# Query projections of a cross attention as seven-product units, with operands made by the output projection and partly kept in DRAM

## The chip, the cores and the metric

One core of one Trainium2 chip runs the whole program. The metric is the device time of one execution in microseconds (us), smaller being better. The engines are TensorE (PE: matmuls; PEld: its weight loads), VectorE (DVE), ScalarE (ACT), GpSimd (POOL) and SyncE (SP), which issues nearly all transfers from one queue, in order.

## The reference, cut to what matters

One layer of a trunk, D = 1024, 1024 tokens, in float32. The part that is changed is the output projection of the mixing block and the cross attention behind it:

```python
x = x + merged @ w_out[i].astype(dt)
h = rmsnorm(x, norm_xattn_g[i])
m = rmsnorm(mem.astype(dt), norm_mem_g[i])
q = (h @ xattn_wq[i].astype(dt)).reshape(bsz, seq, XATTN_HEADS, XATTN_HEAD_DIM)
...
s = jnp.einsum('bshd,bmhd->bhsm', q, k).astype(f32) * (XATTN_HEAD_DIM ** -0.5)
p = jax.nn.softmax(s, axis=-1).astype(dt)
o = jnp.einsum('bhsm,bmhd->bshd', p, v).reshape(bsz, seq, D_MODEL)
x = x + o @ xattn_wo[i].astype(dt)
```

There are 4 heads of 256 columns and 256 memory tokens. In front of this stand two recurrent branches and their merge, behind it a squared-ReLU MLP and a last norm.

## The kernel before

**Arithmetic.** Everything is feature-major: a tile has 128 features as partitions and 512 tokens (a *half*) as its free axis, and x is 8 blocks by 2 halves, in the slots A0a (half 0) and A0b (half 1). A float32 product is made of three fp32r matmuls (`mm3`, L519, L521, L523): both operands are split in a rounded high part (`split`: ACT, L559) and a low rest (DVE or POOL, L560), and high x high, high x low and low x high are summed in PSUM.

**Units of seven products.** The branch projections, the attention's output projection (`pu` below) and the MLP take 256 output columns and all 1024 tokens as a 2x2 problem of blocks and use a Winograd form of Strassen's scheme: seven products p = 0 to 6 of 4 blocks of 128 each, so 7 x 4 x 3 = 84 matmuls of 512 columns for what otherwise takes 96. `wino_w` makes the seven weight operands (sums, then splits, into tiles `wop`, a ring of 4); `blocks` makes the seven operands of the other side from four blocks b00, b01, b10, b11 (row block, half): it sinks b00 (0), b10 (1), b11 (5), then overwrites in place b11-b01 (4), b01-b00 (3), their sum T (2) and b10-T (6). `direct` splits an operand into its slot at once, `spill` writes it to DRAM, from where `load_op` reads it into a small staging tile (`rawa`, two buffers, or `e`) and splits it.

**The output projection** (`phase_out`) is plain: per unit u of 256 columns 96 matmuls; L1875 adds a block to x, L1876 writes the high part of g*x (ACT) and L1859 the low part (DVE), straight into the operand slots of the queries, and the squares for the norm are summed (L624 to L628). The norm's factor is applied later, in the softmax (`rsc`).

**The attention** (`phase_attn`). `queries(h, half)` makes one head's queries for one half: 48 matmuls in 2 blocks of 128, evicted and split (L1920, L1921) into `qt`, which is slot B0b. These eight generators are the *fill*: `scores(h, g)` emits, for each of four blocks of 128 tokens, six matmuls of 256 columns and a softmax (L1947 to L1955), then `SF` = 11 fill matmuls. Within it `flush` finishes the group before: transposes of the probabilities (L591), their split (L1931, L1932), `PF0` = 4 fill matmuls, 12 matmuls with v, and the blocks of the result (L1940) go to `pd` in DRAM (heads 0 to 2) or into the operand slots (head 3). Half 0 of head 0 is made ahead of the first scores; the other seven half-heads fill the groups up to and with scores(3, 0). Scores(3, 1), the eighth group, has none. Then `pu` runs, two units at a time, each twice 84 matmuls; `into_x` (L1707, L1712, L1719) adds to x, and its operand slots are A1a, A1b, B0a, t4, B0b, B1a, B1b. B0b, B1a and B1b hold `qt`, the transposed probabilities and the keys and values until the last flush.

**Order.** The program is traced once; then `Plan` simulates all engines with costs per instruction and writes an order for each engine by due times (four rounds, the best is kept). On PE it takes the earliest traced matmul that is ready, so later matmuls move into gaps; two-input sums marked as flexible go to DVE or POOL. On the chip each engine then runs its list in order.

Of the kernel before, what the change touches and what calls it, by code (L numbers as in the profile page):

```python
# [18 lines left out]
P = 128  # L19
# [29 lines left out]
SF, PF0 = 11, 4  # L49

# [399 lines left out]
class Layer:  # L450
# [186 lines left out]
    def consts(self):  # L637
# [22 lines left out]
        self.gneg = self.til(cp, [P, NB, GH], "gneg")  # L660
# [186 lines left out]
    def decay_cols(self, gb):  # L847
        nc = self.nc
        pt = self.pss()
        for c in range(NB):  # L850
            nc.tensor.transpose(pt[:, c * 64:(c + 1) * 64], gb[:, c * P:(c + 1) * P], self.ident[:64, :64])
        nc.vector.tensor_copy(self.tm, pt.rearrange("p (a b c) -> p a b c", b=2, c=32)[:, :, :, 0:GH])
        nc.scalar.activation(self.geg, self.tm[:, :, 0], AF.Exp)
        nc.vector.tensor_scalar(self.gneg, self.geg, -1.0, None, MUL)
# [354 lines left out]
    def gdn_keys(self, sp, sq, h, st):  # L1209
# [14 lines left out]
        nb = self.til(sq, [P, NB], "nb", bufs=2)  # L1224
# [107 lines left out]
    def gdn_scan(self, sp, hs, sts, nfill):  # L1332
# [4 lines left out]
        for c in range(NB):  # L1337
            zh, qs, dl, pd = {}, {}, {}, {}
            for h, st in hs:
# [8 lines left out]
                nc.vector.scalar_tensor_tensor(zh[h], pa[:, 0:P], self.gneg[:, c, h:h + 1], v[:, c, :], MUL, ADD)  # L1348
# [4 lines left out]
            for h, st in hs:  # L1353
# [3 lines left out]
                nc.scalar.activation(dl[h], py[:, 0:P], AF.Copy, scale=st["b"][:, c:c + 1])  # L1357
# [164 lines left out]
    def op_tile(self, ops, p):  # L1522

        if p not in ops:
            n = self.SL[p]
            ops[p] = self.til(self.lp, [P, 2, 4, HALF], n, F32R, bufs=1) if n == "t4" else self.slot(n, (2, 4, HALF))
# [6 lines left out]
    def staged(self, sp, src, both=True):  # L1533
# [5 lines left out]
        return raw  # L1539

# [310 lines left out]
    def phase_out(self, sp):  # L1851
# [3 lines left out]
        h2 = self.h2 = {}  # L1855

        def lo_in(blk, half):
            g, x = self.g_x[:, blk:blk + 1], self.xT[half][:, blk]
            nc.vector.scalar_tensor_tensor(h2[half][1][:, blk], x, g, h2[half][0][:, blk].bitcast(F32), MUL, SUB)  # L1859

        h2[0] = [self.slot("A1a"), self.slot("A1b")]
        h2[1] = [self.til(self.lp, [P, 2, 4, HALF], "t4", F32R, bufs=1).rearrange("p a b t -> p (a b) t")]

        def out(u):
            w = self.plain_w()
            yield
            for i in range(2):
                blk = 2 * u + i
                for half in range(2):
                    hi, lo = self.mT[half]  # L1870
                    pt = self.psd()
                    yield from self.mm3(pt, [((w[i, b % 2][:, 0, b // 2], w[i, b % 2][:, 1, b // 2]), (hi[:, b], lo[:, b]))
                                             for b in (0, 1, 2, 3, 4, 6, 5, 7)])
                    x = self.xT[half][:, blk]
                    nc.vector.scalar_tensor_tensor(x, pt, 0.5, x, MUL, ADD)  # L1875
                    nc.scalar.activation(h2[half][0][:, blk], x, AF.Copy, scale=self.g_x[:, blk:blk + 1])  # L1876
                    if half == 0:
                        lo_in(blk, half)
                    sq(blk, half)
# [4 lines left out]
        h2[1].append(self.slot("B0a"))  # L1884
        for blk in range(NB):
            lo_in(blk, 1)


    def phase_attn(self, sp):
        nc = self.nc  # L1890
        sc = 1.0 / 16.0
        h2 = self.h2
        rs, pend, puts, op = {}, [], {}, {}
        pd = lambda p, k: self.pd[p][:, k]
        self.SL = ("A1a", "A1b", "B0a", "t4", "B0b", "B1a", "B1b")
        qt, pT, kv = self.slot("B0b", (2, 2, 2, HALF)), self.slot("B1a", (2, 2, 2, HALF)), self.slot("B1b", (2, 2, 2, 2, MEM))
# [11 lines left out]
        qw = {}  # L1908

        def queries(h, half):  # L1910
            if half == 0:
                qw[h] = self.plain_w()
            w = qw[h]
            for i in range(2):
                hi, lo = h2[half]
                pt = self.psd()
                yield from self.mm3(pt, [((w[i, b % 2][:, 0, b // 2], w[i, b % 2][:, 1, b // 2]), (hi[:, b], lo[:, b]))
                                         for b in (0, 1, 2, 3, 4, 6, 5, 7)])
                q = qt[:, half, :, i]
                nc.scalar.activation(q[:, 0], pt, AF.Copy)  # L1920
                nc.vector.tensor_tensor(q[:, 1], pt, q[:, 0].bitcast(F32), SUB)  # L1921

        def flush():
# [3 lines left out]
            n = (2 * h + g) % 2  # L1927
            for mb in range(2):
                pt = self.transpose4([e[:, mb * P:(mb + 1) * P] for e in ps])
                t = pT[:, n, :, mb]  # L1930
# [4 lines left out]
            for i in range(2):  # L1935
                pt = self.psd()
                fs = slice(i * P, (i + 1) * P)
                self.all3(pt, [((v[:, 0, mb, fs], v[:, 1, mb, fs]), (pT[:, n, 0, mb], pT[:, n, 1, mb])) for mb in range(2)])
# [21 lines left out]
        def scores(h, g):  # L1960
            k, ps = kv[:, 0, h % 2], []
            for i in range(4):
                pt = self.pss()
                ts = slice(i * P, (i + 1) * P)
                self.all3(pt[:, :MEM], [((qt[:, g, 0, b, ts], qt[:, g, 1, b, ts]), (k[:, 0, b], k[:, 1, b])) for b in range(2)])
# [6 lines left out]
        for h in range(XH):  # L1972
            for half in range(2):
                self.push(f"q{h}{half}", queries(h, half))
# [4 lines left out]
        self.until("q00")  # L1979
        for h in range(XH):  # L1980
            for g in range(2):
# [3 lines left out]
                self.until(f"q{h + g}{1 - g}")  # L1985
                if h == XH - 1:
                    for p in ((0, 1, 2), (3,))[g]:
                        self.load_op(sp, op, p, pd, range(XH - 1), False)
        self.mo = {}
# [14 lines left out]

        flush()
        for p in (4, 5, 6):
            self.load_op(sp, op, p, pd, range(XH - 1), False)
# [257 lines left out]
    def run(self):  # L2265
# [11 lines left out]
        self.gcd = dt([GH, T], "gcd")  # L2277
        self.dmd = [dt([P, T], f"dmd{h}") for h in range(GH)]
# [44 lines left out]
        with ExitStack():  # L2323
            self.phase_merge(sp, ob)
            self.phase_out(sp)
# [100 lines left out]
```

## Time and profile before

| | |
|---|---|
| Time, median of 3 runs (lowest to highest) | 2171.57 us (2170.28 to 2173.66) |
| Profiled execution: time / span | 2173.49 us / 2171.7 us |
| PE, DVE, ACT, POOL busy | 98%, 76%, 51%, 8% of the span |
| DMA, mean | 142 GB/s |
| Output projection / attention / `pu` | about 1232 to 1314 / 1314 to 1462 / 1462 to 1541 us |

The span runs from the first to the last instruction; the profiled execution took 1.8 us more than its span. A busy PE is not PE at its peak, since matmuls overlap: the pitch from start to start counts, not the length of one.

### The profile page before, as it was taken

What the parts mean: (1) busy time and instruction counts of PE and PEld (TensorE: products, weight loads), DVE (VectorE), ACT (ScalarE), POOL (GpSimd) and SP (SyncE); (2) the same over time, 40 slices, a digit from 0 to 9 for tenths busy, and PEclk for the clock granted to TensorE, in tenths of its full rate; (3) what the DMA queues carried; (4) which work ended last, traced back from release to release, by engine and by line L of the source; (5) the groups of instructions that cost most, each with busy time, mean ns of one, the idle gap of its engine ahead of it and who ended that gap; (6) DMA issues with size and microseconds to landing.
All of it is one profiled execution on the core that took longest, in us unless ns stands there. A gap on an engine that the chain in (4) does not pass through costs nothing. (4 is left out here: it accounts for less than half of the span.)

```text
span 2171.7 us, 31058 instructions
## 1 busy us (share of the span) xinstructions
PE 2138.2 (98%) x11064; PEld 1811.3 (83%) x11064; DVE 1660.2 (76%) x3001; ACT 1103.3 (51%) x2199; POOL 181.4 (8%) x209
## 2 busy tenths in 40 slices
PE   8999999999999999999999999999999999999998
PEld 7789889888888888888888888887888888888877
DVE  7869988885778879685689844469989778567766
ACT  6445545543656464655444434565655556444433
POOL 0001010101112110210000000001101000000011
PEclk9999999999999999999999999999999999999999
DMA  8422323223121211221768621345354445688852
GB/s 303 178 74 94 109 93 127 88 83 134 38 69 64 78 55 48 63 84 63 263 225 303 223 97 62 112 151 172 116 190 129 159 156 178 194 266 287 279 184 93
DMA packets 145308, 308.54 MB, mean 142 GB/s; under 512 B 15865, under 2 KB 19321, under 8 KB 145153
## 3 DMA queue, kind: packets, MB, share of 16 engines
q1 hardware_dynamic: 142256, 302.33, 42.5%
q10 hardware_dynamic: 2896, 4.22, 0.5%
q8 instruction: 87, 1.43, 0.3%
q14 instruction: 69, 0.56, 0.1%
HBM read 216.54 MB, written 89.95 MB: 141 GB/s over the span
## 5 line engine op out<-in xcount | busy, mean ns | idle before, releaser
L559 ACT ACTIVATE wop<-raw 128x512 fp32r<-128x512 f32 (+1 forms) x465 | 303.5, 659 | 469.8 <-PE pd L523 223.9
L560 DVE TENSOR_TENSOR wop<-raw,wop 128x512 fp32r<-128x512 f32 (+1 forms) x439 | 316.0, 723 | 117.1 <-ACT wop L559 111.0
L523 PE MATMUL pd<-t,wop 128*128 128x512 f32 x296 | 117.7, 397 | 0.2 <-DVE wop L560 0.2
L519 PE MATMUL pd<-t,wop 128*128 128x512 f32 x296 | 115.9, 391 | 1.2 <-DVE u L1707 1.2
L523 PE MATMUL pd<-A1a,wop 128*128 128x512 f32 (+1 forms) x292 | 111.1, 381 | 0.0
L519 PE MATMUL pd<-A1a,wop 128*128 128x512 f32 (+1 forms) x292 | 111.0, 380 | 0.0
L1174 DVE SCALAR_TENSOR_TENSOR acc<-cin,convw,acc 128x1024 f32<-128x1024 f32 x72 | 92.2, 1280 | 5.1 <-ACT acc L1172 4.7
L521 PE MATMUL pd<-t,wop 128*128 128x512 f32 x232 | 90.5, 390 | 0.0
L521 PE MATMUL pd<-A1a,wop 128*128 128x512 f32 (+1 forms) x228 | 85.5, 375 | 0.0
L521 PE MATMUL pd<-A1b,wop 128*128 128x512 f32 x212 | 83.1, 392 | 0.0
L560 DVE TENSOR_TENSOR wlo<-raw,whi 128x512 fp32r<-128x512 f32 x59 | 40.2, 687 | 42.2 <-ACT whi L559 41.4
L521 PE MATMUL pd<-B0a,wop 128*128 128x512 f32 x176 | 69.0, 392 | 0.0
L559 ACT ACTIVATE whi<-raw 128x512 fp32r<-128x512 f32 x68 | 41.9, 627 | 52.7 <-PE pd L521 45.4
L519 PE MATMUL pd<-B0a,wop 128*128 128x512 f32 x176 | 68.6, 390 | 0.0
L523 PE MATMUL pd<-B0a,wop 128*128 128x512 f32 x176 | 68.6, 390 | 0.0
L521 PE MATMUL pd<-B0b,wop 128*128 128x512 f32 x176 | 68.5, 389 | 0.0
L521 PE MATMUL pd<-B1b,wop 128*128 128x512 f32 x172 | 66.9, 389 | 0.0
L519 PEld LDWEIGHTS pd<-t,wop 128*128 128x128 f32 x296 | 55.7, 188 | 12.5 <-DVE u L1707 2.0
L523 PEld LDWEIGHTS pd<-t,wop 128*128 128x128 f32 x296 | 55.7, 188 | 11.6 <-DVE wop L560 0.7
L519 PEld LDWEIGHTS pd<-A1a,wop 128*128 128x128 f32 x292 | 55.1, 189 | 9.8
L523 PEld LDWEIGHTS pd<-A1a,wop 128*128 128x128 f32 x292 | 55.0, 188 | 9.6
L1171 ACT ACTIVATE cin<-pd 128x512 f32<-128x512 f32 x48 | 28.5, 594 | 67.5 <-PE pd L523 67.4
(613 smaller groups left out, 6676.0 us busy)
## 6 DMA issues: line engine op xcount, KB each, us to landing
raw<-in_w_dram SPq DMA_DIRECT2D x120, 256.0 KB, 3.7
raw<-in_w_dram SPq DMA_DIRECT2D x32, 512.0 KB, 4.2
e<-ad SPq DMA_DIRECT2D x63, 256.0 KB, 4.4
raw<-in_w_gdn_dram SPq DMA_DIRECT2D x48, 256.0 KB, 2.8
ad<-q SPq DMA_DIRECT2D x45, 256.0 KB, 3.0
rawa<-ad SPq DMA_DIRECT2D x42, 256.0 KB, 4.1
A0b<-tgd SPq DMA_DIRECT2D x32, 256.0 KB, 5.0
ad<-acc SPq DMA_DIRECT2D x30, 256.0 KB, 3.1
```

The source lines that it names most:

```text
L519: nc.tensor.matmul(out, lh, rh, start=first and i == 0, stop=False)
L521: nc.tensor.matmul(out, lh, rl, start=False, stop=False)
L523: nc.tensor.matmul(out, ll, rh, start=False, stop=last and i == n - 1)
L559: nc.scalar.activation(hi, raw, AF.Copy)
L560: (lo_eng or nc.gpsimd).tensor_tensor(lo, raw, hi.bitcast(F32), SUB)
L1171: nc.scalar.activation(cin[:, 4 + half * HALF:4 + (half + 1) * HALF], pt, AF.Copy)
L1174: nc.vector.scalar_tensor_tensor(acc, cin[:, 1 + i:1 + i + T], cw[:, i:i + 1], acc, MUL, ADD)
```

## The change

The queries become units of seven products, one per head (84 matmuls in place of 96). Their operands are sums of blocks of g*x, which the output projection makes with `blocks` as it goes: operands 0 to 3 are split into slots (2 in a new tile `x4`), 4 to 6 go to DRAM (`qd`) and are read back behind the last matmul of the projection. x goes to DRAM as well (`xd`) and is read back for `pu`, because its slots now hold the queries and the transposed probabilities. A head's queries are added up from the products and split by `put_q`, and the queries of head h+1 are the fill of both groups of head h; scores(3, 0) has no fill any more. `pu` finds all its operand slots free once the queries of head 3 are made, and reads its operands through four staging buffers (`late_op`). In the recurrent branch a sign is moved into a scale, which drops the small tile `gneg`.

```diff
@@ -47,6 +47,7 @@
...
+QLOV = (0, 2, 5)
...
@@ -851,7 +851,6 @@
...
-        nc.vector.tensor_scalar(self.gneg, self.geg, -1.0, None, MUL)
...
@@ -1345,7 +1344,7 @@
...
-                nc.vector.scalar_tensor_tensor(zh[h], pa[:, 0:P], self.gneg[:, c, h:h + 1], v[:, c, :], MUL, ADD)
+                nc.vector.scalar_tensor_tensor(zh[h], pa[:, 0:P], self.geg[:, c, h:h + 1], v[:, c, :], MUL, SUB)
@@ -1354,7 +1353,7 @@
...
-                nc.scalar.activation(dl[h], py[:, 0:P], AF.Copy, scale=st["b"][:, c:c + 1])
+                nc.scalar.activation(dl[h], py[:, 0:P], AF.Copy, scale=st["nb" if c else "b"][:, c:c + 1])
@@ -1522,8 +1521,9 @@
...
-            n = self.SL[p]
-            ops[p] = self.til(self.lp, [P, 2, 4, HALF], n, F32R, bufs=1) if n == "t4" else self.slot(n, (2, 4, HALF))
+            n = ops.get("SL", self.SL)[p]
+            pool = self.lp if n == "t4" else self.xp if n == "x4" else None
+            ops[p] = self.til(pool, [P, 2, 4, HALF], n, F32R, bufs=1) if pool else self.slot(n, (2, 4, HALF))
@@ -1537,6 +1537,13 @@
...
+
+    def late_op(self, sp, ops, p, src, ks):
+        for k in ks:
+            self.nraw += 1
+            raw = self.til(sp, [P, HALF], "acc", bufs=2) if self.nraw % 2 else self.til(self.lp, [P, HALF], "rawa", bufs=2)
+            self.load(raw, src(p, k))
+            self.put_op(ops, p, k, raw)
@@ -1852,48 +1859,56 @@
...
         sq = self.sq_sum(sp)
-        h2 = self.h2 = {}
...
+        qo = self.qo = {"SL": self.QL}
+
+        def operand(u):
+
+            def sink(p, x):
+                if p in self.QL4:
+                    nc.sync.dma_start(self.qd[p][:, u], x)
+                else:
+                    self.put_op(qo, p, u, x)
+
+            return self.blocks(sink, nc.gpsimd, False)
...
             w = self.plain_w()
+            put = operand(u)
             yield
-            for i in range(2):
+            for i, half in ((0, 0), (0, 1), (1, 0), (1, 1)) if u < 3 else ((0, 0), (1, 0), (0, 1), (1, 1)):
                 blk = 2 * u + i
...
+                x = self.xT[half][:, blk]
+                nc.vector.scalar_tensor_tensor(x, pt, 0.5, x, MUL, ADD)
+                nc.sync.dma_start(self.xd[half][:, blk], x)
+                t = self.til(sp, [P, HALF], "q", bufs=4)
+                nc.scalar.activation(t, x, AF.Copy, scale=self.g_x[:, blk:blk + 1])
+                sq(blk, half)
+                put(i, half, t)
...
         self.drain()
-        h2[1].append(self.slot("B0a"))
-        for blk in range(NB):
-            lo_in(blk, 1)
-
+        for p in self.QL4:
+            self.load_op(sp, qo, p, lambda p, k: self.qd[p][:, k], range(4))
+
+
+    QL, QL4 = ("A1a", "A1b", "x4", "t4", "B0a", "B0b", "B1a"), (4, 5, 6)
...
         sc = 1.0 / 16.0
-        h2 = self.h2
-        rs, pend, puts, op = {}, [], {}, {}
+        qo = self.qo
+        rs, pend, puts, op = {}, [], {}, {"SL": self.QL}
         pd = lambda p, k: self.pd[p][:, k]
-        self.SL = ("A1a", "A1b", "B0a", "t4", "B0b", "B1a", "B1b")
-        qt, pT, kv = self.slot("B0b", (2, 2, 2, HALF)), self.slot("B1a", (2, 2, 2, HALF)), self.slot("B1b", (2, 2, 2, 2, MEM))
+        self.SL = self.QL[:2] + ("B1b",) + self.QL[3:]
+        qt, pq, kv = self.slot("A0a", (4, 2, HALF)), self.slot("A0b", (2, 2, 2, HALF)), self.slot("B1b", (2, 2, 2, 2, MEM))
+        pT, room = pq[:, 0], [qt[:, i] for i in range(4)] + [pq[:, 1, 0]]
+        held = [self.til(self.wp, [P, HALF], "u", bufs=3) for _ in range(3)]
+        home = {}
@@ -1905,29 +1920,55 @@
...
-        qw = {}
-
...
+        made = {}
+
+        def queries(h):
+            n, (w,) = self.wino_w(range(7), QLOV)
+            t = made[h] = {}
+            yield
+
+            def add(o, pt, x):
+                nc.vector.tensor_tensor(o, pt, x, ADD)
+
+            for p in range(7):
+                if p == 3:
+                    self.fetch_w()
                 pt = self.psd()
...
+                yield from self.mm3(pt, [((w[p][0][:, k], w[p][1][:, k]), (qo[p][:, 0, k], qo[p][:, 1, k])) for k in range(n)])
+                if p == 0:
+                    t[1, 0], t[0, 1], t[1, 1] = held
+                    u = t[1, 0]
+                    nc.scalar.activation(u, pt, AF.Copy)
+                elif p == 1:
+                    add(t[0, 1], pt, u)
+                    home[h, 0, 0] = q = room.pop()
+                    self.split(t[0, 1], q[:, 0], q[:, 1], nc.vector)
+                elif p == 3:
+                    add(t[0, 1], pt, u)
+                elif p == 4:
+                    add(t[1, 1], pt, t[0, 1])
+                    add(u, pt, u)
+                elif p == 5:
+                    add(t[0, 1], pt, t[0, 1])
+                else:
+                    add(u, pt, u)
+
+        def put_q(h):
+            if h:
+                room.extend(home[h - 1, i, half] for i in range(2) for half in range(2))
+            for i, half in ((1, 0), (0, 1), (1, 1)):
+                home[h, i, half] = q = room.pop()
+                self.split(made[h][i, half], q[:, 0], q[:, 1], nc.vector)
+            if h < XH - 1:
+                self.push(f"q{h + 1}", queries(h + 1))
...
                 puts[h] = self.spill(self.pd, h) if h < XH - 1 else self.direct(op, h)
-            n = (2 * h + g) % 2
             for mb in range(2):
                 pt = self.transpose4([e[:, mb * P:(mb + 1) * P] for e in ps])
-                t = pT[:, n, :, mb]
+                t = pT[:, :, mb]
                 nc.scalar.activation(t[:, 0], pt, AF.Copy)
@@ -1962,31 +2003,32 @@
...
                 ts = slice(i * P, (i + 1) * P)
-                self.all3(pt[:, :MEM], [((qt[:, g, 0, b, ts], qt[:, g, 1, b, ts]), (k[:, 0, b], k[:, 1, b])) for b in range(2)])
+                self.all3(pt[:, :MEM], [((home[h, b, g][:, 0, ts], home[h, b, g][:, 1, ts]), (k[:, 0, b], k[:, 1, b])) for b in range(2)])
                 softmax(g, i, pt, ps)
...
-        for h in range(XH):
-            for half in range(2):
-                self.push(f"q{h}{half}", queries(h, half))
+        self.push("q0", queries(0))
         for h in range(2):
...
         scales(0)
-        self.until("q00")
+        self.until("q0")
+        put_q(0)
         for h in range(XH):
...
                 scores(h, g)
-                self.until(f"q{h + g}{1 - g}")
+                if g and h < XH - 1:
+                    self.until(f"q{h + 1}")
+                    put_q(h + 1)
                 if h == XH - 1:
-                    for p in ((0, 1, 2), (3,))[g]:
-                        self.load_op(sp, op, p, pd, range(XH - 1), False)
-        self.mo = {}
+                    for p in ((0, 1, 2, 3), (4, 5, 6))[g]:
+                        self.late_op(sp, op, p, pd, range(XH - 1))
+        self.mo = {"SL": self.SL}
@@ -2002,9 +2044,15 @@
...
+        x = self.xT = {0: self.slot("A0a", (NB, HALF), F32)}
+        for k in range(0, NB, 2):
+            self.load(x[0][:, k:k + 2], self.xd[0][:, k:k + 2])
         flush()
-        for p in (4, 5, 6):
-            self.load_op(sp, op, p, pd, range(XH - 1), False)
+        x[1] = self.slot("A0b", (NB, HALF), F32)
+        for k in range(1, NB, 2):
+            self.load(x[1][:, k], self.xd[1][:, k])
+        for k in range(0, NB, 2):
+            self.load(x[1][:, k], self.xd[1][:, k])
         self.push("pu", pu((0, 1), [self.spill(self.hd, u, nc.vector) for u in (0, 1)]))
@@ -2275,6 +2323,8 @@
...
+        self.qd = [dt([P, 4, HALF], f"qd{p}") for p in range(7)]
+        self.xd = [dt([P, NB, HALF], f"xd{i}") for i in range(2)]
@@ -2320,8 +2370,9 @@
...
-        with ExitStack():
+        with ExitStack() as ctx:
...
+            self.xp = self.pool(ctx, "xt", "left")
```

## Rows read from the trace of the kernel before

**Rows 1.** Page, part 1: busy time, share of the span and instructions of each engine.
```profile
PE 2138.2 (98%) x11064; PEld 1811.3 (83%) x11064; DVE 1660.2 (76%) x3001; ACT 1103.3 (51%) x2199; POOL 181.4 (8%) x209
```
**Rows 2.** Waits of PE from 1316 to 1600 us: total, times, longest.
```profile
PE pd L519 <- ACT B1b L559: 2.4, 1, 2.4
PE ps L519 <- ACT e L1953: 0.5, 1, 0.5
```
**Rows 3.** Busy time in stretches: PE, PEld, DVE, ACT, POOL; clock, DMA share, GB/s.
```profile
1274.00:1295.00 21.00, 21.00 (x94) 17.38 (x93) 9.58 (x14) 7.51 (x12) 0.00 (x0) 1.00 0.28 93
...
1345.00:1363.00 18.00, 18.00 (x95) 15.19 (x94) 5.79 (x16) 8.48 (x19) 0.00 (x0) 1.00 0.15 45
1363.00:1381.00 18.00, 18.00 (x95) 15.25 (x94) 10.74 (x25) 10.21 (x25) 0.00 (x0) 1.00 0.52 162
```
**Rows 4.** The same, in tens, around the last scores and `pu`.
```profile
1447.00:1457.00 10.00, 9.06 (x50) 7.14 (x49) 6.55 (x19) 7.73 (x21) 3.26 (x2) 1.00 0.37 110
1457.00:1467.00 10.00, 10.00 (x47) 7.99 (x46) 6.68 (x11) 7.50 (x15) 0.00 (x0) 1.00 0.39 104
1467.00:1477.00 10.00, 10.00 (x46) 8.29 (x45) 10.00 (x16) 5.62 (x11) 1.63 (x1) 1.00 0.29 72
...
1487.00:1497.00 10.00, 7.56 (x34) 5.95 (x33) 8.91 (x15) 4.10 (x7) 1.30 (x1) 1.00 0.72 208
...
1587.00:1597.00 10.00, 10.00 (x46) 8.29 (x45) 9.68 (x17) 6.02 (x11) 0.00 (x0) 1.00 0.69 225
```
**Rows 5.** Timeline of PE in the output projection: start, length.
```profile
1237.09 0.39 PE L523 MATMUL pd<-B1a,wop 128*128 128x512 f32 x1
...
1269.05 0.39 PE L523 MATMUL pd<-B1a,wop 128*128 128x512 f32 x1
```
**Rows 6.** Groups of instructions, 1232.5 to 1316 us: busy, mean ns; idle before.
```profile
L559 ACT ACTIVATE wop<-raw 128x512 fp32r<-128x512 f32 x16 | 10.1, 631 | 20.0 <-PE pd L523 17.8 <-issue 2.2
```
**Rows 7.** Groups of DVE, 1316 to 1447 us.
```profile
L1947 DVE TENSOR_REDUCE mx<-ps 128x1 f32<-128x256 f32 x28 | 11.8, 422 | 23.4 <-PE ps L523 23.3
L1921 DVE TENSOR_TENSOR B0b<-pd,B0b 128x512 fp32r<-128x512 f32 x15 | 10.3, 686 | 8.2 <-ACT B0b L1920 8.2
```
**Rows 8.** Timelines: ACT in one softmax; PE just behind the last scores.
```profile
1432.87 0.56 ACT L1953 ACTIVATE e<-ps,mx,rsc 128x256 f32<-128x256 f32 x1
1433.33 0.19 ACT L1953 ACTIVATION_READ_ACCUMULATOR e<-ps,mx,rsc 128x1 f32 x1
1433.76 0.51 ACT L1955 ACTIVATE e<-e,smx 128x256 f32<-128x256 f32 x1 [0.23 <-DVE smx L1954]
...
1452.84 0.94 PE L591 MATMUL ps<-ident,e 128*128 128x128 f32 x4 [0.29 <-ACT e L1955]
```
**Rows 9.** Timeline of DVE, and the one POOL row beside it.
```profile
1467.72 0.69 DVE L560 TENSOR_TENSOR B0b<-rawa,B0b 128x512 fp32r<-128x512 f32 x1
1468.32 1.79 DVE L560 TENSOR_TENSOR wop<-raw,wop 128x512 fp32r<-128x512 f32 x1
...
1467.93 1.63 POOL L1571 TENSOR_TENSOR q<-q,q 128x512 f32<-128x512 f32 x1 [17.68 <-ACT wop L559]
```
**Rows 10.** Transfers of the whole run: count, KB each, median us to landing.
```profile
pd<-q SPq DMA_DIRECT2D x21, 256.0 KB, 3.6
rawa<-pd SPq DMA_DIRECT2D x21, 256.0 KB, 3.2
...
A0a<-in_xT_dram SPq DMA_DIRECT2D x4, 512.0 KB, 6.1
```
**Rows 11.** Timelines of SP and PE where `pu` waits for its last operand.
```profile
1450.74 26.93 SPq L488 DMA_DIRECT2D rawa<-pd  x10
...
1495.85 0.50 PE L519 MATMUL pd<-B1b,wop 128*128 128x512 f32 x1 [2.44 <-ACT B1b L559]
```
**Rows 12.** Timeline where the output projection ends and the queries begin.
```profile
1313.25 0.39 PE L523 MATMUL pd<-B1a,wop 128*128 128x512 f32 x1
...
1313.47 0.39 PE L519 MATMUL pd<-A1a,wop 128*128 128x512 f32 x1
```

More of the change, by code (lines that the diff above doesn't have):

```diff
@@ L659, in consts @@
         self.geg = self.til(cp, [P, NB, GH], "geg")
-        self.gneg = self.til(cp, [P, NB, GH], "gneg")
         self.gge, self.kf = (self.til(cp, [P, GH, NB], n) for n in ("gge", "kf"))
@@ L1223, in gdn_keys @@
         b = st["b"] = self.til(sq, [P, NB], "b", bufs=2)
-        nb = self.til(sq, [P, NB], "nb", bufs=2)
+        nb = st["nb"] = self.til(sq, [P, NB], "nb", bufs=2)
         vs = st["vs"] = self.til(sq, [P, NB], "vs", bufs=2)
@@ L1854, in phase_out @@
         sq = self.sq_sum(sp)
-        h2 = self.h2 = {}
[L1857 to L1862, printed above, removed]
+        qo = self.qo = {"SL": self.QL}
[6 more added lines that the diff above has]
+            return self.blocks(sink, nc.gpsimd, False)
         def out(u):
             w = self.plain_w()
+            put = operand(u)
             yield
-            for i in range(2):
+            for i, half in ((0, 0), (0, 1), (1, 0), (1, 1)) if u < 3 else ((0, 0), (1, 0), (0, 1), (1, 1)):
                 blk = 2 * u + i
-                for half in range(2):
[L1870 to L1879, printed above, removed]
+                hi, lo = self.mT[half]
+                pt = self.psd()
+                yield from self.mm3(pt, [((w[i, b % 2][:, 0, b // 2], w[i, b % 2][:, 1, b // 2]), (hi[:, b], lo[:, b]))
+                                         for b in (0, 1, 2, 3, 4, 6, 5, 7)])
+                x = self.xT[half][:, blk]
[5 more added lines that the diff above has]
+                put(i, half, t)
         for u in range(4):
@@ L1906, in load_kv @@
             self.load(kv[:, 1, h % 2].bitcast(F32), self.Vd[h])
-        qw = {}
[L1910 to L1915, printed above, removed]
-                pt = self.psd()
[L1917 to L1921, printed above, removed]
+        made = {}
[8 more added lines that the diff above has]
+                    self.fetch_w()
+                pt = self.psd()
+                yield from self.mm3(pt, [((w[p][0][:, k], w[p][1][:, k]), (qo[p][:, 0, k], qo[p][:, 1, k])) for k in range(n)])
[24 more added lines that the diff above has]
+                self.push(f"q{h + 1}", queries(h + 1))
         def flush():
@@ L1937, in flush @@
                 fs = slice(i * P, (i + 1) * P)
-                self.all3(pt, [((v[:, 0, mb, fs], v[:, 1, mb, fs]), (pT[:, n, 0, mb], pT[:, n, 1, mb])) for mb in range(2)])
+                self.all3(pt, [((v[:, 0, mb, fs], v[:, 1, mb, fs]), (pT[:, 0, mb], pT[:, 1, mb])) for mb in range(2)])
                 b = self.til(sp, [P, HALF], "q", bufs=4)
@@ L1970, in scores @@
             pend.append((h, g, ps))
-        for h in range(XH):
-            for half in range(2):
-                self.push(f"q{h}{half}", queries(h, half))
+        self.push("q0", queries(0))
         for h in range(2):
```

## Prediction

> **What bounds the kernel now.** I read the page first: PE is busy 98% of the span, the next engine 76% [rows 1]. So time goes down when PE has less to do, as long as nothing else makes it wait. Then the stretches. In the output projection and the attention PE is never idle, while DVE works 9.6 of 21 us there and 16.5 of 36 us in the attention, and ACT 7.5 and 18.7 [rows 3]. Around the last scores and in `pu` it is otherwise: DVE is full in eleven of twelve tens from 1467 us on, and only gets free behind 1587 [rows 4] (the ten tens left out there show 9.9 to 10.0). PE has few waits from 1316 to 1600 us: 2.4 us for the last operand of `pu`, 0.5 and 0.3 us behind the last scores, the one group without fill [rows 2, 8]. Two regions are to be seen: one in which PE alone bounds, with cover to spare, and a second in which DVE runs level with it.
>
> **What it removes.** A matmul of 512 columns has a pitch of 0.227 us: 141 steps in 31.96 us [rows 5]. Four heads times 12 matmuls fewer are 48, so 48 x 0.227 = 10.9 us of PE, in stretches where PE never waits.
>
> **What the projection gets.** Per unit (about 21 us) the four high parts of g*x become four plain copies, so ACT gains the four splits of operands 0 to 3: 4 x 0.63 [rows 6] = 2.5, 10.0 of 21 in all. DVE loses the two low parts of half 0 and gains four low parts and up to four sums, six more operations at 0.69, like the splits in the `pu` stretch [rows 9]: 9.6 + 4.1 = 13.7 of 21. Both hide under the 96 matmuls; without that cover they would cost 4 us a unit. The 16 writes of x and 12 of operands are 7.3 MB in 84 us, 87 GB/s on top of 93, where 225 is seen elsewhere [rows 3, 4]. Some sums are offered to POOL.
>
> One POOL sum took 1.63 us, and the DVE split beside it 1.79 us, where the split before it took 0.69 [rows 9]. So a sum given to POOL still costs DVE 1.1 us, more than doing it; I count all sums as DVE's, and by the other price (44 sums, 48 us over 200) DVE would still fit under the matmuls of these stages. The Trainium skill's GPSIMD Engine Reference (Key points) says that POOL shares its interfaces to SBUF with VectorE and that VectorE is about twice as fast in elementwise work; this trace agrees. It speaks against the change in `pu` alone, where DVE is full.
>
> **The boundary.** Today the first query matmul follows the last one of the projection at the normal pitch [rows 12]. Afterwards the last block must be added, scaled, written to DRAM as operand 5, and only then overwritten for operands 4, 3 and 2. From the last matmul E: adding and scaling take 1.7 us with latencies, the write 3.6 [rows 10], the three sums 0.6 each, a split 1.2: operand 2 is whole at about E + 8.4. Products 0 and 1 keep PE until E + 5.4, and the last block of operand 2 is read nine matmuls later, at E + 7.5. Operand 4 goes through DRAM: subtracted at E + 5.9, written 3.6, read 3.2, split 1.4: E + 14.1, due at E + 12.9. Lateness is 0.9 plus 1.2 at most; but PE may take the first nine matmuls of the three products after a blocked one (four PSUM tiles, ready operands), 6 us of other work. Nothing to +2.1, taken +0.5. The write and read of 256 KB are 6.8 us by rows. The Trainium skill (DMA: Bandwidth & Descriptors, Anatomy of one DMA, written for the GpSimd queue) gives 2.0 us fixed plus bytes over 436 GB/s and warns of long receipts from HBM; by it the pair would take an estimated 5.2 us, and the sum would be the same.
>
> **The attention.** A head's queries now cost DVE seven adds from PSUM (0.69 each, as an eviction there [rows 7]), three more weight splits and up to four weight sums: 14 x 0.6 to 0.69, about 9 us; ACT gets four more operations, 2.5 us. Against 36 - 2.7 = 33.3 us a head that is 25.5 for DVE and 21 for ACT: hidden, and price nothing. Between heads the new queries need an add and a split (2.4 us) before the next scores; the next head's product 0 is ready work for that gap, as its weights and operands lie there.
>
> **The last scores.** Scores(3, 0) loses its fill, so two groups and three flushes stand uncovered instead of one group and two flushes. The one group costs 0.8 us of PE today [rows 2, 8], because the first products of `pu` move in. They will again: 36 matmuls over blocks 0 to 2 of operands 0 and 1 (8.2 us), bounded by the ring of four weight tiles. Needed: the softmax of a tile takes ACT 0.56 + 0.19 + 0.51 = 1.26 us [rows 8] against 0.7 us of its six matmuls at half the pitch, so a group lags by 4 x 0.56 = 2.2 us and its flush by 1.5 more. Bounds: nothing, and 3.7 + 1.5 = +5; taken +2, nearer to the row. The transposed probabilities also lose their second buffer; a group of scores lies between two flushes, so this is priced at nothing.
>
> **`pu`.** Today ten operand loads take 26.9 us, 2.7 us each, through two staging buffers, and B1b, free only after the last flush, is 2.4 us late [rows 11]. Afterwards all seven slots are free when the last query is made, and there are four buffers: -2.4 (or nothing, if DVE sets the pace). x comes back as 12 transfers; its first piece takes some 6 us [rows 10], while PE has eight PSUM tiles (21.8 us) before it must wait.
>
> DVE is what is left. From 1447 to 1587 us it worked 132 us, while PE had 136.6 us of work and 3.4 of waits [rows 4]. Without the fill of scores(3, 0) the same stretch gets four softmaxes (4 x 0.8, half of it the maximum [rows 7]), two splits and three sums of a flush (5 x 0.6) and three query splits (3 x 0.6): 8 us for DVE, and about 5 of scores and flush for PE. That makes 140 against 141.6. That is level, so any unevenness is lost. Bounds: 0, if work moves to before the stretch, and +6, if seven operand splits (4.2) that run under fill today and 2 us of gaps come on top; taken +2.5, near the balance.
>
> The sign edit swaps operations of the same kind and takes out one small one; it is priced at nothing. The written order is made anew for the whole program; no row prices that.
>
> **Sum.** -10.9 + 0.5 + 2 - 2.4 + 2.5 = -8.3 us. The profiled execution took 2173.5 (span 2171.7 and 1.8 around it), so 2165.2; the median of the runs is 1.9 us below it: 2163.3. I forecast 2163, a range of its own of 2159 to 2167.
>
> **The rivals.**
> *Given back.* Last scores and `pu` both cost their upper ends and the late operand stays: -10.9 + 0.5 + 5 + 6 = +0.6 at the worst, half of that about -5; middle 2168.5. For it: DVE at 10.0 of 10 [rows 4]. Against it: PE stays at 10.0 beside it.
> *All of it.* Nothing is lost anywhere: -10.9 - 2.4 = -13.3, so 2158. For it: cover everywhere else [rows 3]; against it: the lost fill.
> *Slower: the queue of SP.* x is traced behind all 21 operand loads on one in-order queue. If the 11 that are left when the last scores end go first at a pace of p, x's first piece lands 11p + 6.1 us later, and DVE, in order, stands behind it; PE has work for about 24 us from there. The loss is 11p - 18: nothing at 1.35 us (four buffers), 11.7 at today's 2.7 (2172), slower than no change by over 0.2% from 3.0 us on; at 3.5 it is 20.5, so 2180. For it: transfers already wait in turn [rows 11]. Against it: SP's order is written by due times, so x may go ahead.
> *No effect of the counts* is excluded: the matmuls are 48 fewer whatever else happens.
>
> **Chances.** My forecast 0.55, all of it 0.15, given back 0.2, the queue 0.1. Measurements tell about 0.2% (4.3 us) from no change: below 2167.2 is faster, above 2175.9 slower. Faster: 0.55 + 0.15 + a quarter of given back = 0.75; slower 0.08 from the queue; the rest, 0.17, same. The range leaves out the lower part of "all of it" and the upper ends of the others: 2157 to 2172.
>
> **What would show it.** The profile after should have 48 matmuls fewer and PE full from the projection to the third head. Right about the boundary: PE waits for B0a to B1a or x4 below 1 us in total; wrong: waits of 2 us and more there. Right about the end of the attention: waits of PE for softmax results (`e`) or the transposed probabilities of 1 to 4 us, `pu` without the wait for B1b, and DVE full earlier than 1467 less the time saved. The queue would show as DVE waiting for x from DRAM. The prediction is wrong if PE loses more than 6 us between the last queries and the end of `pu`, or if the new order loses time in stages that the change doesn't touch.

## The result, and the profile after

The changed kernel takes 2177.74 us (median of 20 runs, 2172.82 to 2180.61), the kernel before 2173.91 beside it (20 runs, 2168.22 to 2178.92). The ratio is 1.0016, with a 95% interval of 1.0009 to 1.0023: 2 to 5 us slower, not 8 us faster, and less than the 4.3 us that I called the limit of telling. The profiled execution took 2179.4 us, its span 2177.7.

The page, part 1 (busy time, share of the span, instructions), beside [rows 1]:

```profile
PE 2134.0 (98%) x11016; PEld 1802.9 (83%) x11016; DVE 1707.3 (78%) x3082; ACT 1123.2 (52%) x2243; POOL 189.1 (9%) x211
```

The 48 matmuls are gone, and yet the span grew by 6.0 us. PE is busy 4.2 us less, so it waits 10 us more. The view of PE's waits from 1316 to 1600 us (total, times, longest), beside [rows 2]:

```profile
PE pd L520 <- ACT B0a L560: 5.5, 1, 5.5
PE pd L520 <- ACT B1a L560: 1.3, 1, 1.3
PE ps L592 <- ACT e L1996: 0.5, 1, 0.5
...
PE pd L522 <- DVE B1b L561: 0.4, 1, 0.4
```

The long wait is new: PE stands for B0a, the slot of operand 4 of the queries. The wait for the last operand of `pu` (B1b, 2.4 us) is down to 0.4. The timeline of PE shows the boundary, beside [rows 12], and the stretch behind the wait, beside [rows 5]:

```profile
1311.21 0.39 PE L524 MATMUL pd<-B1a,wop 128*128 128x512 f32 x1
1311.43 0.39 PE L520 MATMUL pd<-A1a,wop 128*128 128x512 f32 x1
...
1326.76 0.28 PE L520 MATMUL ps<-B1b,A0b 128*128 128x256 f32 x1
...
1332.82 0.79 PE L520 MATMUL pd<-B0a,wop 128*128 128x512 f32 x1 [5.54 <-ACT B0a L560]
...
1334.57 0.63 PE L520 MATMUL pd<-B0b,wop 128*128 128x512 f32 x1
...
1338.40 0.63 PE L520 MATMUL pd<-B0b,wop 128*128 128x512 f32 x1
1338.83 0.58 PE L522 MATMUL pd<-B0b,wop 128*128 128x512 f32 x1
1339.25 0.40 PE L524 MATMUL pd<-B0b,wop 128*128 128x512 f32 x1
1340.95 0.50 PE L520 MATMUL pd<-B1a,wop 128*128 128x512 f32 x1 [1.30 <-ACT B1a L560]
```

The handover itself has the normal pitch. PE then takes what is ready, the first scores among it (the 256-column rows, with keys in B1b); behind 1327 the next matmul in its order needs the last block of operand 4, and product 5 (B0b) comes only after it. Behind the wait the pitch is 0.43 us in place of 0.227. The table of stretches shows the granted clock beside it (columns as in [rows 3]):

```profile
1320.00:1330.00 10.00, 7.27 (x36) 5.48 (x34) 8.39 (x15) 4.54 (x8) 1.01 (x1) 1.00 0.83 255
1330.00:1335.00 5.00, 2.18 (x5) 1.34 (x6) 4.28 (x12) 1.31 (x3) 0.00 (x0) 0.74 0.73 265
1335.00:1340.00 5.00, 4.65 (x12) 3.29 (x11) 3.37 (x7) 1.78 (x4) 0.00 (x0) 0.58 0.80 247
1340.00:1345.00 5.00, 4.05 (x18) 3.30 (x19) 3.48 (x6) 2.46 (x5) 0.00 (x0) 1.00 0.00 0
```

The granted clock falls to 0.58, near the lower level of 1.2 GHz; some 15 matmuls at 0.2 us more each are another 3 us. And the DMA columns read 0.73 to 0.83 busy at 247 to 265 GB/s. The view of the chain that ended last (start, us, what) follows the late block, from the write of operand 5 (line 1) and the sum that overwrites its buffer (line 2) to the write, the read and the split of operand 4:

```profile
1313.77 5.52 DMA qd<-q
...
1319.92 0.70 DVE q L1570
...
1320.63 3.59 DMA qd<-q
...
1324.24 7.88 DMA rawa<-qd
...
1332.14 0.64 ACT B0a L560
```

SP's issues in the same time, without these two writes:

```profile
1321.23 1.52 SPq L489 DMA_DIRECT2D e<-qd  x2
1322.80 0.43 SPq L489 DMA_DIRECT2D raw<-in_xq_dram  x1
1323.28 0.43 SPq L489 DMA_DIRECT2D B1b<-Kd  x1
1324.24 1.01 SPq L489 DMA_DIRECT2D rawa<-qd  x2
1325.65 0.32 SPq L1868 DMA_DIRECT2D qd<-q  x1
1326.03 0.50 SPq L489 DMA_DIRECT2D e<-qd  x1
```

Operand 5's write took 5.5 us, not 3.6, and the sum that overwrites its buffer started 6.1 us after the write's issue: the write had landed at 1319.29, and DVE finished another split first. Operand 4's write took 3.6 us, as I had it; its read took 7.9 us, where I took 3.2. The transfers of 1300 to 1345 us (KB each, median us from issue to landing) agree, beside [rows 10]:

```profile
e<-qd SPq DMA_DIRECT2D x8, 256.0 KB, 5.5
qd<-q SPq DMA_DIRECT2D x4, 256.0 KB, 4.6
...
rawa<-qd SPq DMA_DIRECT2D x4, 256.0 KB, 7.9
```

From 1321.2 to 1326.0 SP issues six reads and writes of 256 KB and 512 KB of weights and of keys each, 2.6 MB in all. At 260 GB/s that takes 10 us, and the late block stands in the middle of it.

One more place lost time, in a stage that the change doesn't touch: the second product of the MLP, 1880 to 2125 us. PE's waits there after, and the one line of before:

```profile
PE pd L524 <- DVE wop L561: 2.3, 1, 2.3
PE pd L520 <- ACT wop L560: 1.7, 3, 0.9
PE pd L520 <- DVE u L1714: 1.3, 1, 1.3
```
```profile
PE pd L519 <- DVE u L1707: 1.2, 2, 1.0
```

**The balance.** I took the length of each stretch and subtracted its matmuls, each at its undisturbed pitch (0.227 us, 0.119 with 256 columns, 0.109 for a transpose, some 0.06 for a one-column sum of the norm). What remains is lost time, in us:

| kernel | boundary 1300–1345 | attention 1345–1465 | `pu` 1465–1550 | MLP 1880–2125 |
|---|---|---|---|---|
| before | 1.0 | 4.0 | 2.7 | 1.8 |
| after | 11.4 | 7.0 | 0.7 | 9.0 |
| difference | +10.4 | +3.0 | −2.0 | +7.3 |

The 48 matmuls give −10.9, and the first 130 us were 1.9 shorter in this execution (they differ by that much between executions of any kernel). Together +5.9, against 6.0 in the spans.

### The profile page after: what moved, and what is told of

The parts are those of the page before. It is cut to its first block, busy times and chain, and to the rows that moved or that the text cites. A ratio compares the mean times of both kernels' runs of the same rounds, so it can differ in the third digit from the quotient of the medians.

```text
span 2177.7 us, 31223 instructions
## 1 busy us (share of the span) xinstructions
PE 2134.0 (98%) x11016; PEld 1802.9 (83%) x11016; DVE 1707.3 (78%) x3082; ACT 1123.2 (52%) x2243; POOL 189.1 (9%) x211
## 4 chain that ended last, share of the span: by engine, by line
PE 69%; DVE 16%; DMA 6%; ACT 4%; issue 3%; SPq 0%; DVEq 0%; POOL 0%; ACTq 0%; POOLq 0%
PE pd L522 16%; PE pd L524 16%; PE pd L520 16%; PE ps L520 4%; PE ps L522 4%; PE ps L524 4%; DVE wop L561 2%; DVE acc L1173 2%; PE ps L1314 1%; DMA raw<-in_w_dram 1%; DVE pr L1279 1%; DVE Pm L1281 1%; PE ps L592 1%; DMA rawa<-ad 1%; DMA e<-ad 1%
## 5 line engine op out<-in xcount | busy, mean ns | idle before, releaser
L560 ACT ACTIVATE wop<-raw 128x512 fp32r<-128x512 f32 (+1 forms) x477 | 310.4, 657 | 464.3 <-PE pd L524 220.9
L561 DVE TENSOR_TENSOR wop<-raw,wop 128x512 fp32r<-128x512 f32 (+1 forms) x449 | 322.9, 723 | 105.8 <-ACT wop L560 99.9
L524 PE MATMUL pd<-t,wop 128*128 128x512 f32 x248 | 99.6, 402 | 2.5 <-DVE wop L561 2.5
L520 PE MATMUL pd<-t,wop 128*128 128x512 f32 x248 | 97.7, 394 | 1.8 <-DVE u L1714 1.3
L522 PE MATMUL pd<-t,wop 128*128 128x512 f32 x248 | 97.5, 393 | 0.0
L520 PE MATMUL pd<-A1a,wop 128*128 128x512 f32 (+1 forms) x244 | 92.1, 377 | 0.9 <-ACT wop L560 0.9
L524 PE MATMUL pd<-A1a,wop 128*128 128x512 f32 (+1 forms) x244 | 92.4, 379 | 0.0
L522 PE MATMUL pd<-A1a,wop 128*128 128x512 f32 (+1 forms) x244 | 91.8, 376 | 0.0
L520 PE MATMUL pd<-B0a,wop 128*128 128x512 f32 x192 | 75.2, 392 | 5.5 <-ACT B0a L560 5.5
L524 PE MATMUL pd<-B0a,wop 128*128 128x512 f32 x192 | 75.0, 391 | 0.0
L520 PE MATMUL pd<-B1a,wop 128*128 128x512 f32 x188 | 73.3, 390 | 1.3 <-ACT B1a L560 1.3
L524 PE MATMUL pd<-B1a,wop 128*128 128x512 f32 x188 | 73.2, 389 | 0.0
L520 PE MATMUL pd<-A1b,wop 128*128 128x512 f32 x164 | 64.2, 392 | 1.5 <-ACT A1b L560 1.5
L524 PE MATMUL pd<-A1b,wop 128*128 128x512 f32 x164 | 64.0, 390 | 0.0
L522 PE MATMUL pd<-A1b,wop 128*128 128x512 f32 x164 | 63.8, 389 | 0.0
L524 PEld LDWEIGHTS pd<-t,wop 128*128 128x128 f32 x248 | 47.0, 190 | 12.9 <-DVE wop L561 3.4
L520 PEld LDWEIGHTS pd<-t,wop 128*128 128x128 f32 x248 | 47.0, 190 | 12.3 <-DVE u L1714 1.6
```

Source lines behind the costliest of these rows:

```text
L520: nc.tensor.matmul(out, lh, rh, start=first and i == 0, stop=False)
L522: nc.tensor.matmul(out, lh, rl, start=False, stop=False)
L524: nc.tensor.matmul(out, ll, rh, start=False, stop=last and i == n - 1)
L560: nc.scalar.activation(hi, raw, AF.Copy)
L561: (lo_eng or nc.gpsimd).tensor_tensor(lo, raw, hi.bitcast(F32), SUB)
```

## The experiments

**Both kernels again.** The changed kernel and the kernel before, unchanged.

> The changed kernel once more, for a second profile. In the first one, counted from equal places in PE's list of matmuls, the boundary between the output projection and the queries cost 9.8 us (waits of 5.5 and 1.3 us, and 3 us of matmuls at the lower clock) and the MLP's second product 7.4 us. Theory 1 (the last unit's operands come too late through DRAM): PE waits for B0a and B1a again, 5 to 9 us together. Theory 2 (the new order or the new alternation of staging buffers costs the MLP's second product time): its waits for weight operands and the sums, 4 to 5 us, come back. Rival (both are chance of one execution): waits below 2 us in either place. Time 1.001 to 1.003 of the kernel before.

> The kernel before once more, for a second profile of it. In the MLP's second product the changed kernel and its variants lost 1.6 to 7.4 us against the one profile of the kernel before, counted from equal places in PE's list. If that is the new order (theory 3), the second profile of the kernel before agrees with its first within 1 us there: waits of PE of about 1.2 us. Rival (this stage varies by several us from execution to execution in any kernel): a loss of 2 us or more.

The changed kernel: 2177.40 us, ratio 1.002 (1.001 to 1.0029), the same waits (5.49 for B0a, 1.30 for B1a), lost times 10.7, 6.8, 0.0, 5.4. The kernel before: 2173.62 in one run, lost times 1.0, 3.5, 2.9, 0. The boundary repeats to 0.7 us; of the MLP's 7.3, 5.4 are there again.

**No last block through DRAM.** The blocks that the last unit of the projection makes of operands 4, 5 and 6 are split straight into their slots; those of the first three units still go through DRAM. (The last line keeps the staging buffers' turn as it was.)

```diff
-                if p in self.QL4:
+                if p in self.QL4 and u < 3:
...
-            self.load_op(sp, qo, p, lambda p, k: self.qd[p][:, k], range(4))
+            self.load_op(sp, qo, p, lambda p, k: self.qd[p][:, k], range(3))
...
+        self.nraw += 3
```

> The changed kernel, but the last unit of the output projection splits its operands 4 to 6 straight into their slots, with no way through DRAM; the nine pieces of the units before still go through it. Theory 1 (the round trip of the last unit is what PE waits for): the waits for B0a and B1a and the stretch at the lower clock go, 8 to 10 us less than the changed kernel, ratio to the kernel before 0.997 to 0.998. Rival (the slots are late in any case, because all twelve reads crowd the queue and the splits crowd ACT and DVE): less than 3 us gained, ratio 1.000 to 1.002.

2166.11 us, ratio 0.9969 (0.9956 to 0.9982). PE's waits from 1300 to 1346 us are these two, and the clock stays at 1.00:

```profile
PE ps L520 <- ACT A0a L560: 0.4, 1, 0.4
PE pd L522 <- DVE B1a L561: 0.2, 1, 0.2
```

The boundary loses 1.4 us, as before the change (1.0). The way of the last blocks through DRAM is the cause of the 10 us there, and of the sign of the result.

**The turn of the staging buffers.** The change shifts which of two kinds of buffer each later operand is staged in; the rival cause for losses behind the attention. It was shifted back in the changed kernel (`self.nraw -= 12` behind the attention), in the direct version (−9), and shifted in the kernel before (+12).

> The changed kernel, but the counter that deals staged loads out to the two kinds of staging buffer is set back by the 12 loads that the change adds, so that the MLP's second product uses the buffers in the same turn as in the kernel before. Theory 2: the 7 us that this stage lost come back, ratio to the kernel before 0.998 to 0.999. Rival (the stage's loss is chance of one execution, or comes from the new order alone): no change against the changed kernel, ratio 1.001 to 1.002.

> Both edits: the last unit's operands split directly, and the counter set back. If theories 1 and 2 hold, their gains add up: 13 to 17 us less than the changed kernel, ratio to the kernel before 0.994 to 0.996. If only theory 1 holds: as with the direct split alone, 0.997 to 0.998.

> The kernel before, with the counter of staged loads set forward by 12 ahead of the MLP, so that its staging buffers alternate as in the changed kernel; nothing else differs. Setting the counter back in the changed kernel gave nothing, so no change is expected: ratio 0.999 to 1.001, waits of PE in the MLP's second product 1 to 3 us. If this alternation is what costs the changed kernel its 3 to 4 us there (rival): ratio 1.0015 to 1.003.

2176.45 (1.0012, 1.0001 to 1.0024), 2167.35 (0.9971, 0.9962 to 0.998), 2173.9 (0.9998, 0.9989 to 1.0007): each as its kernel without the shift. The MLP's stage lost 5.6, 6.7 and 0 us. This rival falls.

**The wait for operand 5's write taken away.** Its last block is copied first, and the copy is written, so that the sum can overwrite at once.

```diff
                 if p in self.QL4:
+                    if p == 5 and u == 3:
+                        y = self.til(sp, [P, HALF], "e", bufs=3)
+                        nc.scalar.activation(y, x, AF.Copy)
+                        x = y
                     nc.sync.dma_start(self.qd[p][:, u], x)
```

> The changed kernel, all operands 4 to 6 through DRAM as there, but for the last unit operand 5 goes out from a copy that ACT makes (0.6 us), so that the subtraction that makes operands 4, 3 and 2 does not have to wait until the write has landed (6.1 us in the profile). If that wait inside the chain is the larger part of the lateness: PE's wait for B0a falls from 5.5 to below 1 us, the lower clock goes with it, and 7 to 10 us are gained, ratio 0.998 to 0.999. If the way back through DRAM (8 us under this load) decides: the chain is shorter by 5 us at most and PE still waits 1 to 4 us; ratio 0.999 to 1.001.

2176.31 us, ratio 1.0014 (1.0004 to 1.0024). PE's waits, 1300 to 1346 us:

```profile
PE pd L520 <- ACT B1a L560: 2.3, 1, 2.3
PE pd L522 <- DVE B0b L561: 1.9, 2, 1.7
PE pd L520 <- ACT B0a L560: 1.1, 1, 1.1
PE pd L520 <- ACT B0b L560: 0.5, 1, 0.5
```

The wait for operand 4 shrinks from 5.5 to 1.1, and operands 5 and 6 (B0b, B1a) become late in its place; the boundary still loses 10.4. An earlier start of the trip only moves the wait.

**Only operand 4 direct.** Its last block alone is split into its slot; those of 5 and 6 still go through DRAM.

```diff
-                if p in self.QL4:
+                if p in self.QL4 and (p != 4 or u < 3):
...
-            self.load_op(sp, qo, p, lambda p, k: self.qd[p][:, k], range(4))
+            self.load_op(sp, qo, p, lambda p, k: self.qd[p][:, k], range(3 if p == 4 else 4))
...
+        self.nraw += 1
```

> The changed kernel, but the last block of operand 4 alone is split straight into its slot; the last blocks of operands 5 and 6 still go through DRAM. Theory A (each way through DRAM under load is late by its own length, and operand 4's only comes first): no wait for B0a; the way of operand 5 (written at about 1314, landed at 1320, read in 8 us, split 1.4: 1329) and of operand 6 (written at about 1322, read back at about 1335) come next, with waits of PE of 2 to 4 us together for B0b and B1a, and less of half clock behind them; the loss from 1300 to 1345 us falls from 10.5 to 3 to 6, the time to 2169 to 2173. Theory B (operand 4 alone is the fault, the later two have cover): the loss there falls to 1.5, as where all three are direct, and the time to 2166 to 2168. Theory C (the in-place overwrite that waits for the write of operand 5 is the fault, whatever goes through DRAM): wait of 4 us and more for x4 or B0a, time not below 2175.

2164.89 us, ratio 0.9958 (0.9945 to 0.9971). The profiled execution was the longest of its five, 2170.3. PE's waits and the transfers in the same stretch:

```profile
PE pd L520 <- ACT t L560: 0.3, 1, 0.3
PE pd L520 <- ACT B1a L560: 0.2, 1, 0.2
```
```profile
e<-qd SPq DMA_DIRECT2D x7, 256.0 KB, 5.2
...
qd<-q SPq DMA_DIRECT2D x4, 256.0 KB, 5.8
...
rawa<-qd SPq DMA_DIRECT2D x2, 256.0 KB, 3.1
```

Theory B holds: the boundary loses 2.0 us. Theory C falls, since here too the in-place sum (1323.04) comes 6.4 us behind the issue of operand 5's write (1316.60, landed at 1322.47), and PE does not stand for it. The writes and the reads into `e` are as slow as before (the two reads at 3.1 us were issued at 1305 and 1310, ahead of the crowd). Operands 5 and 6 are in time once operand 4 is whole; the likely reason is that its last matmuls and the work behind them then run meanwhile. So one block of 256 KB, the one whose use comes first and whose making comes second, carried nearly the whole loss: 2.0 us are left of 11.4.

**Even fill.** 4 x 11 + 4 = 48 fill matmuls a group were a half-head of queries; now a head has 84, 42 a group, and 4 x 10 + 3 = 43. The same edit in five kernels:

```diff
-SF, PF0 = 11, 4
+SF, PF0 = 10, 3
```
With all three operands direct:

> The last unit's operands split directly, and the fill of a block of scores cut from 11 to 10 matmuls and of a flush from 4 to 3, so that a head's 84 matmuls reach the last block of the second group of scores. If the uneven fill is what costs 3 us between the third head and the last flush: 1 to 3 us less than with the direct split alone, ratio 0.995 to 0.9965. If it is scores(3, 0), which has no fill in either: no change, 0.9965 to 0.9975.

In the changed kernel:

> The changed kernel with the fill counts 10 and 3 in place of 11 and 4, nothing else. 4 x 11 + 4 = 48 were the matmuls of a half-head of queries before; the change leaves 84 a head, 42 a group, and 4 x 10 + 3 = 43. If uneven fill costs the attention its 3 us, the loss from 1345 to 1465 us falls from 7 to about 5.5 and the boundary stays at 10 to 11: 2174 to 2177, unless the stage of the MLP's second product also gains from the new written order, as it did with all three operands direct (then 2171 to 2173). If fill counts are worth nothing by themselves: 2177, loss unchanged.

In the kernel before:

> The kernel before with the fill counts 10 and 3: 43 of the 48 matmuls of a half-head in the group, 5 behind it. If even fill is what counts, the kernel before loses by it or stays, 2174 to 2176. If the counts help by the new order alone, in stages that have nothing to do with them, it may come out 1 to 4 us faster: 2170 to 2173.

With operand 4 direct:

> Both edits that helped: the last block of operand 4 straight into its slot, and the fill counts 10 and 3. If the two are independent, the boundary costs 2 us as with operand 4 alone, the last scores 3.5 in place of 5.2, and the time is 1.5 to 3 us below that of operand 4 alone: 2161 to 2164. If the time with operand 4 alone came from a written order that the counts upset (the stage of the MLP's second product lost 0 to 7 us by the order so far), it is 2164 to 2169.

| kernel | time, us | ratio (95%) | attention, lost us | MLP, lost us |
|---|---|---|---|---|
| three direct | 2161.5 | 0.9947 (0.9935 to 0.996) | 6.5 (8.0 without) | 1.3 (3.3 without) |
| changed kernel | 2174.52 | 1.0009 (0.9999 to 1.002) | 6.3 (7.0) | 5.2 (9.0, 5.4) |
| kernel before | 2172.35 | 0.9995 (0.9986 to 1.0005) | 4.4 (4.0) | 0.4 (1.8, 0) |
| operand 4 direct | 2165.67 | 0.9964 (0.9951 to 0.9978) | 6.2 (7.5) | 4.2 (5.6) |

That even fill helps the attention is not shown. With it the new scheme lost 6.2 to 6.5 us there; without it 7.0 and 6.8 (changed kernel), 7.0 (staging shifted back), 8.0 and 7.5 (above), but also 6.4 (three direct, staging shifted back) and 5.7 (copied operand 5). The 8.0 and the 7.5 each hold a stretch at the lower clock that none of the others has (granted 0.78 and 0.88 from 1435 to 1445 us with three direct, 0.66 from 1435 to 1440 with operand 4 direct), worth some 1.7 us. In the old scheme it gives nothing. With operand 4 direct the counts make no difference that the runs tell: the boundary lost 3.2 in place of 2.0. The fastest kernel seen, 2161.5, is 9 to 14 us below the kernel before; its interval overlaps that of operand 4 direct, so the two aren't told apart.

**Where the MLP's stage loses.** No experiment changed that stage alone; the rows show how it happens. DVE and ACT of the changed kernel:

```profile
2089.26 0.69 DVE L561 TENSOR_TENSOR B1a<-e,B1a 128x512 fp32r<-128x512 f32 x1 [2.70 <-ACT B1a L560]
2089.87 1.28 DVE L1714 TENSOR_TENSOR acc<-pd,q 128x512 f32<-128x512 f32 x2
...
2093.08 1.74 DVE L561 TENSOR_TENSOR wop<-raw,wop 128x512 fp32r<-128x512 f32 x1
```
```profile
2088.59 0.63 ACT L560 ACTIVATE B1a<-e 128x512 fp32r<-128x512 f32 x1 [2.76 <-DMA e<-ad]
```

A split of an operand stands ahead of the evictions on DVE, and the operand comes late from DRAM; then evictions and weight splits come in a heap, and PE waits 2.3 us for a weight. The split of that weight took 1.74 us on DVE; up to 2094.27 POOL split other weights beside it, and the pair in [rows 9] showed 1.79 in place of 0.69:

```profile
2091.33 2.94 POOL L561 TENSOR_TENSOR wop<-raw,wop 128x512 fp32r<-128x512 f32 x2
```

Behind the waits the granted clock falls here as well:

```profile
2095.00:2100.00 5.00, 3.70 (x9) 2.66 (x10) 5.00 (x9) 0.00 (x0) 1.28 (x1) 0.70 0.35 109
```

Eight matmuls at 0.2 us more are 1.6 of the 9.0 us. Five more of the ten profiles with seven-product queries have such a stretch in this stage (the changed kernel again, both with staging shifted back, operand 4 direct with and without even fill); the four of the kernel before have none. In the kernel before the same eviction starts at 2085.65, released by PE:

```profile
2085.65 1.37 DVE L1707 TENSOR_TENSOR acc<-pd,q 128x512 f32<-128x512 f32 x2 [1.12 <-PE pd L523]
```

PE's list is the same in all these kernels over the last 2200 matmuls, apart from names of slots; the lists of DVE, ACT and SP differ. The version with all three direct and even fill shares its list of the last 600 DVE instructions to 97% and more with the kernel before with shifted staging, and these two lost 1.3 and 0 us; the changed kernel's matches these two to some 60% (in longest common runs) and lost 9.0 and 5.4. That speaks for the written order, but does not show it: the list of three direct with staging shifted back is as near to that of the kernel before (86%) as these two are (83%), and lost 6.7. And one list can lose unlike amounts: the changed kernel 9.0 and 5.4 in its two profiles, operand 4 direct and all three direct, with the same DVE list there, 5.6 and 3.3, of which 1.6 is the lower clock that only the first had. Over all ten profiles with seven-product queries the stage lost 1.3 to 9.0 us, over the four without 0 to 1.8. Why the new lists are worse here stays open.

## Why the prediction was wrong

The step that failed is **the boundary**: +0.5 us, bound +2.1, measured +10.4. Three things went wrong in it.

- The durations of write (3.6) and read (3.2) are medians over transfers of the whole run [rows 10]. At this place operand 5's write stands among 2.4 MB issued from 1311.4 to 1315.2 us and took 5.5, and operand 4's read among 2.6 MB and took 7.9; operand 4's write took the 3.6. Operand 4 was whole at E + 21.9 (last matmul E = 1311.6, low part done 1333.5) in place of E + 14.1. I had counted 87 GB/s of new traffic over the projection, as an average, and not what falls together behind its end. By the page that I weighed there (the Trainium skill, DMA: Bandwidth & Descriptors, Anatomy of one DMA) one such transfer is an estimated 2.6 us. Its warning of long receipts is for writes into HBM above all, and here it was the read back that was longest. This trace does not separate receipt from queue; 7.9 us for this read, beside 3.1 for reads of the same size ahead of the crowd in another kernel, speak for the queue.
- Of the 6 us of other work behind operand 4, PE had 2.8: 12 score matmuls, the column sums of the norm and small gaps took it from E + 12.9 to 1327.3, that is E + 15.7. The first nine matmuls of product 5, which I had counted, stand behind operand 4's in PE's order and ran only from 1334.57; their blocks came back through the same queue, the second and third split at 1326.78 and 1327.84. The first matmul of operand 4's last block started 8.3 us after it was due, 2.8 of them covered, 5.5 waited. Operand 2 was late too (E + 13.2 in place of 8.4), and there the cover held: PE took matmuls of products 3 and 4 first, and did not wait.
- The granted clock behind a long wait had no price: 0.74 and 0.58 of full speed for 6.5 us, 3 us lost.

The other steps, by the balance:

- **What it removes**: 48 matmuls, 10.9 us, as counted.
- **The projection's cover**: right. PE is full up to the boundary; from 1274 to 1295 us DVE worked 11.9 us and ACT 9.7, against 13.7 and 10.0 worked out.
- **Attention and last scores**: +2 taken, up to +5; measured +3.0, one of them between heads (from 1.2 to 2.0 up to 1420 us) and two at the last scores (2.8 to 5.1). Right in kind and inside its bounds.
- **`pu`**: the late operand is gone, as said (−2.4). DVE's backlog, taken +2.5, cost at most 0.4: the stretch lost 2.0 less than before. From 1447 to 1587 us DVE worked 133.9 us where 140 was worked out (132.0 before). Part of the rest was perhaps done earlier, as my lower bound had it: from 1345 to 1363 us DVE worked 15.0 of 18, where it had worked 5.8 [rows 3] and the queries were to add some 5.
- **The written order** "made anew", with "no row prices that": the MLP's second product, where the change leaves the work as it was, lost 7.3 and 5.4 us more in the two pairs of profiles. That the order is the cause is likely, not shown. I named it as what would make the prediction wrong, and gave it no chance in the range. It does not decide the sign: with the boundary repaired and 3.3 to 5.6 us still lost here, the time lies in the range.
- **The rivals.** *Slower: the queue of SP* names the right kind of mechanism at the wrong place: x went ahead of 12 of the operand loads (its first pieces were issued at 1455.00), and DVE never waited for it. Its times (2172, 2180) are added to the sum without the 2.5 us of `pu`, which its text does not say. *All of it* and *given back* both failed with the boundary.

With the boundary repaired (operand 4 direct, 2164.89; three direct, 2166.11) the change lands 2 and 3 us above the forecast of 2163, and this with the MLP's loss still in it, so partly by offsetting errors.

## What to carry to other kernels

Price a trip through DRAM on the critical path by what else is issued within those microseconds, not by a median of the run; if the bytes queued there take longer than the slack, keep that one block on chip. And count as cover only work whose own operands do not come by the same queue. Of the three spilled blocks here, the one that is used first decided, and sparing it alone gave nearly the whole gain back. When a planner writes a new order for the whole program, compare the lost time of every stage, also of those that were not edited, and leave room for it in the range.

## What the runs showed of the hardware

A wait of 5.5 us was followed by a granted clock of 0.74 and 0.58 in the next two stretches of 5 us and a pitch of 0.43 in place of 0.227. Waits of 0.5 to 2.3 us close together (5.8 us in all from 1328 to 1339, in the version with the copied operand 5) did the same:

```profile
1335.00:1340.00 5.00, 1.79 (x5) 1.16 (x6) 4.27 (x11) 3.23 (x6) 0.00 (x0) 0.77 0.33 131
1340.00:1345.00 5.00, 5.00 (x14) 3.93 (x13) 1.06 (x2) 0.00 (x0) 0.00 (x0) 0.54 0.00 0
```

The length of one wait does not settle it. At the last operand of `pu`, a wait of 2.4 us in the kernel before [rows 4, 11] and of 2.7 in its second profile left the clock at 1.00; one of 2.1 at the same place, in the kernel before with shifted staging, was followed by 0.95 and then 0.70:

```profile
PE pd L519 <- ACT B1b L559: 2.1, 1, 2.1
```
```profile
1500.00:1505.00 5.00, 5.00 (x17) 3.95 (x17) 4.28 (x8) 1.49 (x3) 1.61 (x1) 0.70 0.62 204
```

At the boundary the slow matmuls cost alike in both kernels: its loss, less the waits and the 1.0 of the kernel before, is 3.6 us with 6.8 of waits (11.4 − 6.8 − 1.0) and 3.6 with 5.8 (10.4 − 5.8 − 1.0).
